# Both heads of a pair turned one behind the other in the attention loop, and latent values taken from their bank by VectorE

## The chip, the core and the metric

The kernel runs on one core of a Trainium2 chip. The metric is the device time of one execution in microseconds (us). Engines are named as the profile names them: PE is the matmul engine TensorE, PEld its weight loads, DVE is VectorE, ACT is ScalarE, POOL is GpSimd, and SP issues the DMA transfers.

## What is computed

A residual trunk of four layers over 512 tokens of width 1024: a gated short convolution, a sparse attention in which an indexer chooses 128 keys for each query (layer B below), a multi-head latent attention (layer C), and a second convolution layer. Both attention layers have 16 heads, 64-wide values, and a softmax over the visible key chunks:

```python
def attend(args):                      # dense_chunk_attention, layer C
    q_b, q0 = args
    logits = jnp.einsum("bqhd,bshd->bhqs", q_b, k).astype(jnp.float32) * scale
    mask = chunk_visible(q0 + jnp.arange(QBLOCK, dtype=jnp.int32), k_pos)
    logits = jnp.where(mask[None, None], logits, -jnp.inf)
    p = jax.nn.softmax(logits, axis=-1).astype(v.dtype)
    return jnp.einsum("bhqs,bshd->bqhd", p, v)

# mla_mixer: keys and values come out of one product of the latent vector
kv = (rmsnorm(ckv, kv_lat_norm) @ w_ukv).reshape(bsz, seq, C_HEADS, C_NOPE + C_V)
k_nope, v = kv[..., :C_NOPE], kv[..., C_NOPE:]
...
return (o * jax.nn.silu(z)) @ w_out
```

## The kernel before

Tokens lie in four blocks of 128 (`NT` = 4), features in eight blocks of 128. Weights stream in from HBM by SP (`raw`), ACT rounds them (`whi`, line 161), POOL subtracts (`wlo`, line 163), and a large product is three matmuls, high by high, low by high and high by low (lines 287 to 289).

All instructions are written in a program order, and a list scheduler lays them out on each engine: of the instructions that it takes for ready at a point of its own timeline, the one that is earliest in the program goes first. So program order is a priority and not the final order, and within an engine's queue the order is then fixed. Semaphores between engines follow from the data, and two engines that touch one PSUM bank are ordered.

`attention` (line 620) serves layers B and C. Its jobs are eight pairs of heads, and each pair is cut into six chunks: query blocks 0 and 1, then 2, then 3, for each of the two heads (even chunk: first head; odd chunk: second head). There are N = 48 chunks. The steps of a chunk are:

- `scores`: for both heads at once; score matmuls into the two `s` banks (of one buffer), then DVE (line 655, with the row maximum `mn`), then ACT's exponential with its sum (line 658).
- `normalise`: one DVE reciprocal `rc` for the pair (line 668), then the scaling of the probabilities by POOL for the first head (line 673) and by ACT for the second (line 675).
- `turn`: PE turns the probabilities, block by block, into one of two `pt` banks (line 685), and ACT copies them back (line 690), or DVE for each sixth chunk (line 688).
- `mix`: once in six chunks, 40 PE instructions (line 706) into the single `o` bank, the last chunks' probabilities first; then DVE multiplies by the gate (line 710).
- `filler`: the projections of later heads, and later gates, step by step; `filler.to(cost)` issues steps until the planned cost of a chunk is reached. `Filler` parts are generators; their own turns use the `tr` bank (line 585).

The loop at line 714 takes one chunk per round, with the scores four chunks ahead; the scores are issued in even rounds only. In a round stand, in this order, the mix, the scores, one normalise, one turn and one portion of filler.

In layer C, `keys_values` (line 1036) is part of that filler: for each block of 128 tokens, six matmuls make keys and values of four heads side by side in one bank (tag `pj`, two banks, when the loop runs; `pj` and `pt` ahead of it). `fin` takes them out: the key part by ACT with the token's factor (line 1043), the value part by ACT with the same factor (line 1044), then POOL squares the key part and DVE sums it (line 1047).

Of the kernel before, what the change touches and what calls it, by code (L numbers as in the profile page):

```python
# [13 lines left out]
AF = mybir.ActivationFunctionType  # L14
OP = mybir.AluOpType
# [56 lines left out]
def encoder(ctx: ExitStack, tc: tile.TileContext, a, out, depth=4):  # L72
# [4 lines left out]
    act_e, dve, pool, pe = nc.scalar, nc.vector, nc.gpsimd, nc.tensor  # L77
# [9 lines left out]
    def tile_of(tag, name, shape=(P, S), dtype=F32):  # L87
        return sb.tile(list(shape), dtype, name=name, tag=tag, bufs=BUFS[tag])
# [4 lines left out]
    def tiny(name, n, dtype=F32, tag="tiny"):  # L93
        return sb.tile([P, n], dtype, name=name, tag=tag, bufs=24)

    def bank(name, tag):
        return ps.tile([P, S], F32, name=name, tag=tag, bufs=BANKS[tag])

    def two_banks(name):

        b = ps.tile([P, 2, S], F32, name=name, tag="s", bufs=1)
        return [b[:, 0], b[:, 1]]
# [233 lines left out]
    def tokens_short(group, act, finish, tags):  # L336

        w = [x for _, u in units(group) for x in u]
        for t in range(NT):
            b = bank("pt", tags[t % len(tags)])  # L340
            for k in range(group.nk):
                products(b[:, :group.n], [y[:, t * P:(t + 1) * P] for y in act[k]], w[k], k == 0, k == group.nk - 1)
            finish(t, b)
            yield
# [275 lines left out]
    def attention(jobs, filler):  # L620

        early_turns[0] = False
        chunks = []
        for j in jobs:
            mine = [(j, e, ts) for ts in ([0, 1], [2], [3]) for e in range(2)]
            for i, c in enumerate(mine):
                chunks.append(c + (j["fill"][0] + (j["fill"][1] - j["fill"][0]) * (i + 1) / len(mine),))  # L630
        stage, soft, wide, factors = {}, {}, {}, {}

        def parts(ts):

            o = 0
            for t in ts:
                yield t, slice(o, o + (t + 1) * P)
                o += (t + 1) * P

        def scores(c):  # L640

            j, _, ts = chunks[c][:3]
            if ts[0] == 0:
                filler.through(j["after"])
            banks = two_banks("s")
            n = len(ts)
            for t, w in parts(ts):
                j["scores"]([b[:, w] for b in banks], t)
            ps_ = [tile_of("p", "p") for _ in range(2)]
            mn = [tiny("mn", n, tag="small") for _ in range(2)]  # L650
            sm = tiny("sum", 2 * n, tag="small")
            for e in range(2):
                p = ps_[e]
                for i, (t, w) in enumerate(parts(ts)):
                    dve.tensor_tensor_reduce(out=p[:, w], in0=banks[e][:, w], in1=j["masks"](t), scale=j["qs"](e, t),  # L655
                                             scalar=-GONE, op0=OP.add, op1=OP.min, accum_out=mn[e][:, i:i + 1])
                for i, (t, w) in enumerate(parts(ts)):
                    act_e.activation(p[:, w], p[:, w], AF.Exp, bias=mn[e][:, i:i + 1], scale=-1.0,  # L658
                                     accum_out=sm[:, e * n + i:e * n + i + 1])
                stage[c + e] = p, sm  # L660

        def normalise(c):

            e, ts = chunks[c][1:3]
            p, sm = stage.pop(c)
            if e == 0:
                rc = tiny("rc", 2 * len(ts), tag="small")
                dve.reciprocal(rc, sm)  # L668
                factors[c] = factors[c + 1] = rc
            rc = factors.pop(c)[:, e * len(ts):(e + 1) * len(ts)]  # L670
            for i, (t, w) in enumerate(parts(ts)):
                if e == 0:
                    pool.tensor_scalar(p[:, w], p[:, w], rc[:, i:i + 1], None, op0=OP.mult)  # L673
                else:
                    act_e.activation(p[:, w], p[:, w], AF.Copy, scale=rc[:, i:i + 1])
            soft[c] = p

        def turn(c):

            ts = chunks[c][2]  # L680
            p = soft.pop(c)
            b = bank("pt", "pt")
            n = sum(t + 1 for t in ts) * P
            for i in range(0, n, P):
                pe.transpose(b[:, i:i + P], p[:, i:i + P], ident)  # L685
                clock[0] += 0.11
            if c % 6 == 5:
                dve.tensor_copy(p[:, :n], b[:, :n])
            else:
                act_e.activation(p[:, :n], b[:, :n], AF.Copy)  # L690
            wide[c] = p

        def mix(c):

            j, e, ts = chunks[c][:3]
            if e == 0 or ts[-1] < NT - 1:
                return
            o = bank("o", "o")
            first = True
            for d in (4, 2, 0):  # L700
                x = [wide.pop(c - 5 + d + e) for e in range(2)]
                for t, w in reversed(list(parts(chunks[c - 5 + d][2]))):
                    for kb in range(t + 1):
                        i = w.start + kb * P
                        for e in (1, 0):
                            pe.matmul(o[64 * e:64 * e + 64, t * P:(t + 1) * P], j["v"](e, kb), x[e][:, i:i + P],  # L706
                                      start=first, stop=t == 0)
                            clock[0] += 0.134
                        first = False
            dve.tensor_tensor(j["dst"](), o, j["dst"](), op=OP.mult)  # L710

        N = len(chunks)
        ahead = 4
        for c in range(-ahead, N + 1):
            if c > 0:
                mix(c - 1)
            if c + ahead < N and c % 2 == 0:
                scores(c + ahead)
            if 0 <= c + ahead - 1 < N:
                normalise(c + ahead - 1)  # L720
            if 0 <= c < N:
                turn(c)
            if c + ahead < N:
                filler.to(chunks[c + ahead][3])
        while filler.step():
            pass
        early_turns[0] = True
# [193 lines left out]
    def layer_c(last):  # L921
# [49 lines left out]
        def factor(which, n):  # L971
            p = token_sums(sums[which])
            v = tiny("lv", NT)
            r2 = tiny("lr2", NT)
            pool.tensor_tensor(out=r2, in0=r, in1=r, op=OP.mult)
            dve.tensor_tensor(v, p[:, :NT], r2, op=OP.mult)
            y = small_rsqrt(v, NT, 1.0 / n)
            f = const([P, NT], "f" + which)
            pool.tensor_tensor(out=f, in0=y, in1=r, op=OP.mult)
            return f  # L980

        fkv = factor("kv", 256)
# [53 lines left out]
        def keys_values(g, dst, vals):  # L1036
            sums = tiny("hs", 16)
            ks = [tile_of("gate", "kk", (P, 4, 96)) for _ in range(NT)]

            def fin(t, b):  # L1040
                b3 = b.rearrange("p (h d) -> p h d", d=P)
                x3 = ks[t][:, :, :64]
                act_e.activation(x3, b3[:, :, :64], AF.Copy, scale=fkv[:, t:t + 1])
                act_e.activation(vals[t // 2][:, t % 2], b3[:, :, 64:], AF.Copy, scale=fkv[:, t:t + 1])
                q = tile_of("rp", "qk2", (P, 4, 64))
                pool.tensor_tensor(out=q, in0=x3, in1=x3, op=OP.mult)
                dve.tensor_reduce(sums[:, 4 * t:4 * t + 4], q, axis=AX.X, op=OP.add)

            yield from tokens_short(a["c_ukv"][g], lat["kv"], fin, free(g))
            v = tiny("hv", 16)  # L1050
            pool.tensor_tensor(out=by_head(v), in0=by_head(sums), in1=krs[:, :, None].to_broadcast([P, NT, 4]),
                               op=OP.add)
            y = small_rsqrt(v, 16, 1.0 / 96)
            for t in range(NT):
                x = ks[t]
                yt = y[:, 4 * t:4 * t + 4, None]
                pool.tensor_tensor(out=x[:, :, :64], in0=x[:, :, :64], in1=yt.to_broadcast([P, 4, 64]), op=OP.mult)
                pool.tensor_tensor(out=x[:, :, 64:], in0=krr[:, t, None].to_broadcast([P, 4, 32]),
                                   in1=yt.to_broadcast([P, 4, 32]), op=OP.mult)

            def finish(h):
                to_features(dst[h], lambda t: ks[t][:, h], 96)
            for h in range(4):
                finish(h)
# [152 lines left out]
```

## Time and profile before

| | us |
|---|---|
| median of 3 runs | 1058.24 (1058.1 to 1058.6) |
| profiled execution, its own time | 1058.71 |
| its span, first to last instruction | 1056.9 |
| PE busy in the span | 1044.1 |
| ACT busy in the span | 511.5 |
| DVE busy in the span | 523.6 |
| POOL busy in the span | 678.3 |

Layer B's loop lies at about 372 to 545 us of the span and layer C's at about 645 to 820 us. A row of the timeline gives the start, the length, engine, line, output and inputs, and how many instructions of one kind were merged. Matmuls overlap in the rows: PE's pace is read from start to start, not from the length of one. A row of waits says who waited for whom: the sum, how often, and the longest. The granted clock of PE was 0.998 of full speed (2.4 GHz) over the span.

### The profile page before, as it was taken

What the parts mean: (1) busy time and instruction counts of PE and PEld (TensorE: products, weight loads), DVE (VectorE), ACT (ScalarE), POOL (GpSimd) and SP (SyncE); (2) the same over time, 40 slices, a digit from 0 to 9 for tenths busy, and PEclk for the clock granted to TensorE, in tenths of its full rate; (3) what the DMA queues carried; (4) which work ended last, traced back from release to release, by engine and by line L of the source; (5) the groups of instructions that cost most, each with busy time, mean ns of one, the idle gap of its engine ahead of it and who ended that gap; (6) DMA issues with size and microseconds to landing.
All of it is one profiled execution on the core that took longest, in us unless ns stands there. A gap on an engine that the chain in (4) does not pass through costs nothing.

```text
span 1056.9 us, 16253 instructions
## 1 busy us (share of the span) xinstructions
PE 1044.1 (99%) x6040; PEld 878.9 (83%) x6040; DVE 523.6 (50%) x1074; ACT 511.5 (48%) x1091; POOL 678.3 (64%) x636
## 2 busy tenths in 40 slices
PE   9999999999999999999999999999999999999998
PEld 7888888898898999898888787687777888888886
DVE  6884334335598974443435344444442664443321
ACT  6243223434444467676644446876764533333231
POOL 1546555666378799685538689788743856555552
PEclk9999999999999999999999999999999999999999
DMA  7233333224222221111213220101211333333332
GB/s 238 93 100 100 99 99 92 83 70 120 81 71 80 72 89 41 61 56 46 71 50 105 82 83 23 41 24 60 61 55 46 100 100 101 99 100 100 100 100 79
DMA packets 27295, 86.44 MB, mean 82 GB/s; under 512 B 3408, under 2 KB 4432, under 8 KB 27216
## 3 DMA queue, kind: packets, MB, share of 16 engines
q1 hardware_dynamic: 26928, 85.10, 25.9%
q8 instruction: 47, 0.77, 0.3%
q10 hardware_dynamic: 288, 0.31, 0.1%
q14 instruction: 32, 0.26, 0.1%
HBM read 83.30 MB, written 2.10 MB: 81 GB/s over the span
## 4 chain that ended last, share of the span: by engine, by line
PE 94%; DVE 2%; ACT 1%; POOL 1%; DMA 1%; issue 1%; ACTq 0%; POOLq 0%
PE pa L287 11%; PE pa L288 11%; PE pa L289 11%; PE po L287 6%; PE po L289 6%; PE po L288 6%; PE o L706 4%; PE pt L685 4%; PE s L1083 3%; PE pz L289 2%; PE pz L288 2%; PE pz L287 2%; PE s L296 2%; PE tr L585 2%; PE pq L287 2%; PE pk L288 2%
## 5 line engine op out<-in xcount | busy, mean ns | idle before, releaser
L163 POOL TENSOR_TENSOR wlo<-raw,whi 128x512 fp32r<-128x512 f32 (+4 forms) x320 | 401.4, 1262 | 281.4 <-ACT whi L161 269.4
L161 ACT ACTIVATE whi<-raw 128x512 fp32r<-128x512 f32 (+4 forms) x329 | 196.9, 603 | 328.9 <-PE pa L288 158.4
L288 PE MATMUL pa<-xl,whi 128*128 128x512 f32 x512 | 199.3, 389 | 0.0
L287 PE MATMUL pa<-xh,whi 128*128 128x512 f32 x512 | 198.2, 389 | 0.6 <-ACT xh L370 0.6
L289 PE MATMUL pa<-xh,wlo 128*128 128x512 f32 x512 | 197.6, 389 | 0.0
L287 PEld LDWEIGHTS pa<-xh,whi 128*128 128x128 f32 x512 | 96.0, 188 | 20.6 <-ACT xh L370 0.8
L288 PEld LDWEIGHTS pa<-xl,whi 128*128 128x128 f32 x512 | 96.1, 188 | 20.5 <-DVE xl L373 0.5
L289 PEld LDWEIGHTS pa<-xh,wlo 128*128 128x128 f32 x512 | 96.1, 188 | 20.0
L673 POOL TENSOR_SCALAR p<-p,rc 128x128 f32<-128x128 f32 (+1 forms) x64 | 70.2, 1103 | 45.9 <-DVE rc L668 40.6
L658 ACT ACTIVATE p<-p,mn 128x128 f32<-128x128 f32 (+3 forms) x128 | 71.0, 558 | 17.5 <-DVE mn L655 17.3
L480 DVE TENSOR_TENSOR cg<-pa,R 128x512 f32<-128x512 f32 x16 | 11.0, 690 | 118.5 <-PE pa L289 116.2
L655 DVE CUSTOM_DVE_ANT_0 p<-s,cmask,qs 128x128 f32<-128x128 f32 (+2 forms) x80 | 37.7, 506 | 33.9 <-PE s L1083 20.0
L287 PE MATMUL pz<-xh,whi 128*128 128x512 f32 x128 | 51.4, 401 | 0.0
L289 PE MATMUL pz<-xh,wlo 128*128 128x512 f32 x128 | 50.9, 398 | 0.0
L288 PE MATMUL pz<-xl,whi 128*128 128x512 f32 x128 | 50.4, 394 | 0.0
L288 PE MATMUL po<-xl,whi 128*128 128x512 f32 x128 | 50.1, 391 | 0.0
L288 PE MATMUL po<-glo,whi 128*128 128x512 f32 x128 | 49.8, 389 | 0.0
L282 POOL TENSOR_TENSOR y<-mean,minus_half 128x16 f32<-128x16 f32 (+1 forms) x18 | 49.2, 2732 | 0.8
L287 PE MATMUL po<-xh,whi 128*128 128x512 f32 x128 | 49.5, 400 | 0.0
L287 PE MATMUL po<-ghi,whi 128*128 128x512 f32 x128 | 49.5, 389 | 0.0
L690 ACT ACTIVATE p<-pt 128x384 f32<-128x384 f32 (+1 forms) x80 | 38.6, 510 | 22.0 <-PE pt L685 21.6
L685 PE MATMUL pt<-ident,p 128*128 128x128 f32 x320 | 47.9, 277 | 0.2 <-ACT p L690 0.2
(247 smaller groups left out, 2418.8 us busy)
## 6 DMA issues: line engine op xcount, KB each, us to landing
raw<-in_a_in SPq DMA_DIRECT2D x63, 512.0 KB, 3.9
raw<-in_a_out SPq DMA_DIRECT2D x16, 512.0 KB, 3.9
raw<-in_b_z SPq DMA_DIRECT2D x8, 512.0 KB, 3.5
raw<-in_b_q SPq DMA_DIRECT2D x8, 512.0 KB, 3.4
raw<-in_b_k SPq DMA_DIRECT2D x8, 512.0 KB, 3.7
raw<-in_b_v SPq DMA_DIRECT2D x8, 512.0 KB, 3.6
raw<-in_c_z SPq DMA_DIRECT2D x8, 512.0 KB, 3.6
raw<-in_b_out SPq DMA_DIRECT2D x8, 384.0 KB, 3.3
```

The costliest lines, as they stand in the source:

```text
L161: act_e.activation(hi[:, :, c], raw[:, j:j + m, c], AF.Copy)
L163: e.tensor_tensor(out=lo, in0=raw[:, j:j + m, :n - few], in1=hi[:, :, :n - few].bitcast(F32), op=OP.subtract)
L282: pool.tensor_tensor(out=y, in0=m, in1=minus_half[:, :n], op=OP.pow)
L287: nc.tensor.matmul(o, l[0], r[0], start=first, stop=False)
L288: nc.tensor.matmul(o, l[0], r[1], start=False, stop=False)
L289: nc.tensor.matmul(o, l[1], r[0], start=False, stop=last)
L655: dve.tensor_tensor_reduce(out=p[:, w], in0=banks[e][:, w], in1=j["masks"](t), scale=j["qs"](e, t), scalar=-GONE, op0=OP.add, op1=OP.min, ...
L658: act_e.activation(p[:, w], p[:, w], AF.Exp, bias=mn[e][:, i:i + 1], scale=-1.0, accum_out=sm[:, e * n + i:e * n + i + 1])
L673: pool.tensor_scalar(p[:, w], p[:, w], rc[:, i:i + 1], None, op0=OP.mult)
L685: pe.transpose(b[:, i:i + P], p[:, i:i + P], ident)
L690: act_e.activation(p[:, :n], b[:, :n], AF.Copy)
L706: pe.matmul(o[64 * e:64 * e + 64, t * P:(t + 1) * P], j["v"](e, kb), x[e][:, i:i + P], start=first, stop=t == 0)
```

## The change

Two edits. The loop of `attention` takes both chunks of a pair in one round: it counts in steps of two, issues the scores of the pair four chunks ahead, normalises the two chunks two and three ahead, turns both chunks of the pair one behind the other, and then issues the filler up to the planned cost of the second chunk of the pair whose scores it issued. In `keys_values` the value part is taken out of its bank by DVE and no longer by ACT.

```diff
         N = len(chunks)
         ahead = 4
-        for c in range(-ahead, N + 1):
+        for c in range(-ahead, N + 1, 2):
             if c > 0:
                 mix(c - 1)
-            if c + ahead < N and c % 2 == 0:
+            if c + ahead < N:
                 scores(c + ahead)
-            if 0 <= c + ahead - 1 < N:
-                normalise(c + ahead - 1)
+            for d in (c + ahead - 2, c + ahead - 1):
+                if 0 <= d < N:
+                    normalise(d)
             if 0 <= c < N:
                 turn(c)
+                turn(c + 1)
             if c + ahead < N:
-                filler.to(chunks[c + ahead][3])
+                filler.to(chunks[c + ahead + 1][3])
         while filler.step():
             pass
         early_turns[0] = True
...
                 act_e.activation(x3, b3[:, :, :64], AF.Copy, scale=fkv[:, t:t + 1])
-                act_e.activation(vals[t // 2][:, t % 2], b3[:, :, 64:], AF.Copy, scale=fkv[:, t:t + 1])
+                dve.tensor_scalar(vals[t // 2][:, t % 2], b3[:, :, 64:], fkv[:, t:t + 1], None, op0=OP.mult)
                 q = tile_of("rp", "qk2", (P, 4, 64))
```

## Rows read from the trace of the kernel before

**Rows 1.** The page's first part: busy us, share of the span, instructions.

```profile
PE 1044.1 (99%) x6040; PEld 878.9 (83%) x6040; DVE 523.6 (50%) x1074; ACT 511.5 (48%) x1091; POOL 678.3 (64%) x636
```

**Rows 2.** Busy us by stretch: length, PE, PEld, DVE, ACT, POOL, clock, DMA.

```profile
372.00:545.00 173.00, 172.60 (x1445) 151.41 (x1443) 81.15 (x235) 114.18 (x286) 126.98 (x115) 1.00 0.19 59
645.00:820.00 175.00, 171.53 (x1094) 135.95 (x1094) 76.05 (x243) 119.92 (x314) 121.79 (x147) 1.00 0.15 44
```

**Rows 3.** Waits, whole span: who for whom, us in total, times, longest.

```profile
PE tr L585 <- ACT kT L113: 1.6, 2, 1.0
PE s L1083 <- DVE mn L655: 1.5, 2, 1.1
...
PEld pt L287 <- ACT v L1044: 0.2, 1, 0.2
...
DVE rc L668 <- ACT p L658: 34.9, 30, 2.0
```

**Rows 4.** PE's timeline in B: start, us, instruction; last-block scores, cut and whole.

```profile
424.33 0.73 PE L296 MATMUL s<-kT,qT 64*128 64x512 f32 x3
424.99 2.40 PE L706 MATMUL o<-p,v 128*64 128x128 f32 x40
427.33 0.73 PE L296 MATMUL s<-kT,qT 64*128 64x512 f32 x3
427.99 0.88 PE L685 MATMUL pt<-ident,p 128*128 128x128 f32 x6
...
484.64 0.96 PE L296 MATMUL s<-kT,qT 64*128 64x512 f32 x5
...
511.69 0.96 PE L296 MATMUL s<-kT,qT 64*128 64x512 f32 x6
512.58 0.33 PE L685 MATMUL pt<-ident,p 128*128 128x128 f32 x1
```

**Rows 5.** PE's timeline in C: a mix in two pieces.

```profile
757.76 1.09 PE L706 MATMUL o<-p,v 128*64 128x128 f32 x14
...
759.35 1.74 PE L706 MATMUL o<-p,v 128*64 128x128 f32 x26
761.02 0.55 PE L685 MATMUL pt<-ident,p 128*128 128x128 f32 x3
```

**Rows 6.** Busy us of line 706 alone: B's and C's loop, one mix of C.

```profile
372.00:545.00 173.00, 19.43 (x320) 17.26 (x320) 1.00 0.19 59
645.00:820.00 175.00, 22.23 (x320) 18.37 (x320) 1.00 0.15 44
...
712.50:720.40 7.90, 3.66 (x40) 2.49 (x40) 1.00 0.42 135
```

**Rows 7.** Chain that ended last: runs of eight turns, first and last of thirteen.

```profile
403.02 1.02 PE pt L685 x8
...
808.19 0.87 PE pt L685 x8
```

**Rows 8.** Groups by line: count, busy us, mean ns, idle before and its releaser.

```profile
L673 POOL TENSOR_SCALAR p<-p,rc 128x128 f32<-128x128 f32 (+1 forms) x64 | 70.2, 1103 | 45.9 <-DVE rc L668 40.6
L690 ACT ACTIVATE p<-pt 128x384 f32<-128x384 f32 (+1 forms) x80 | 38.6, 510 | 22.0 <-PE pt L685 21.6
...
L1044 ACT ACTIVATE v<-pt,fkv 128x256 f32<-128x256 f32 x16 | 7.4, 470 | 0.0
L1018 DVE TENSOR_TENSOR qk<-pt,gqk 128x256 f32<-128x256 f32 x16 | 6.7, 420 | 7.3 <-ACT qk L1017 7.3
```

**Rows 9.** Timeline in C's loop: ends of two key-and-value blocks, copies between.

```profile
721.64 0.39 PE L289 MATMUL pt<-whi,llo 128*128 128x512 f32 x1
...
722.07 0.47 ACT L1043 ACTIVATE kk<-pt,fkv 128x256 f32<-128x256 f32 x1 [1.40 <-PE pt L289]
...
722.44 0.46 ACT L1044 ACTIVATE v<-pt,fkv 128x256 f32<-128x256 f32 x1
...
723.00 0.39 PE L289 MATMUL pt<-whi,llo 128*128 128x512 f32 x1
```

## Prediction

> **What bounds the kernel now.** I read the busy table first: the matmul row of TensorE (PE) is busy for 1044.1 of 1056.9 us, every other engine for 64% of the span or less [rows 1]. A busy row alone does not say that the engine is at its pace, so the second view is the table by stages. The change touches two stretches: the attention loop of the sparse layer (B, 372 to 545 us) and that of the latent layer (C, 645 to 820 us). PE is without work for 173.00 - 172.60 = 0.4 us of the first and 175.00 - 171.53 = 3.5 us of the second; VectorE (DVE) is busy for under half of either, ScalarE (ACT) for two thirds [rows 2]. The third view is PE's waits: over the whole kernel the named ones are small, among them 1.5 us for DVE's `mn` (the score banks) and 1.6 us for ACT's `kT` (the `tr` bank); PE's weight loads waited 0.2 us for ACT's `v` [rows 3].
>
> So the loop is not held up by its attention chain. The scheduler fills every wait with other matmuls, those of the filler first. What such a kernel can still lose lies in the order of PE's own stream: runs of one kind that are cut in two. That is the fourth view, PE's instructions in order. In B the six score matmuls of the last query block take 512.58 - 511.69 = 0.89 us when they run through. At 424 us the scheduler puts the mix (40 instructions) into their middle: three take 424.99 - 424.33 = 0.66 us, and the other three, behind the mix, 427.99 - 427.33 = 0.66 us, so 1.32 us in all. One cut costs 0.43 us. B has four such places, at 424, 445, 465 and 485 us [rows 4]. A mix can be cut as well. Whole, as at 424.99, it is busy for 2.40 us and takes 2.34 until PE's next start [rows 4]. In C one goes through in pieces of 14 and 26, with four turns of the filler between: the pieces are busy for 1.09 + 1.74 = 2.83 us, and take 2.69 from start to next start (1.02 for the first, up to the filler's turns, and 761.02 - 759.35 = 1.67 for the second), so a cut costs some 0.36 us [rows 5]. The eight mixes of B are busy for 19.43 us, the eight of C for 22.23, against 8 x 2.40 = 19.2 [rows 6]: nearly all cuts of mixes are C's.
>
> **The change part by part.** Nothing is removed from PE: the same scores, turns, mixes and filler are issued. What moves is the program order, which gives the scheduler its priorities.
>
> *Both turns together, the filler behind them.* So far a pair's second turn stood behind one portion of filler, and the mix behind one more. Now both turns stand ahead of a double portion, and mix and scores follow it. Turns beside each other save nothing as such: thirteen runs of eight turns (five in B, eight in C) are already whole, the first of them 1.02 us from start to next start, the last 0.87 [rows 7]. What changes is how early the mix can start. Its last input is the second head's copy, and that is now due a whole double portion before it. At the four places of B the scores went first although they stand behind the mix in the program, so the scheduler took the mix for not yet ready. With the copies earlier I expect mix, then scores, unbroken: 4 x 0.43 = **1.7 us less**. Bounds: 1.7 us less at best, and 1.7 us more if instead the other four pairs of B are cut, at the same price.
>
> *Normalising one portion later.* The even head's scaling on GpSimd (POOL) now stands behind the whole portion of filler, together with the odd head's on ACT; the turn follows one double portion later, not three single ones. In the queue of POOL this puts the filler's low-part subtractions ahead of a scaling of 1.10 us. POOL stood still ahead of these scalings for 40.6 us, waiting for the reciprocal [rows 8], and DVE for 34.9 us over 30 waits ahead of the reciprocal, for the exponentials [rows 3]. Part of this goes, but PE did not wait for it, so I cost it at nothing. Its cover is the double portion, in B on average 173/24 = 7.2 us a pair; if it ran out, one scaling (1.10 us) would show per pair that it concerns.
>
> *Banks and tiles.* The two turns of a pair take both `pt` banks at once, each freed by a copy (0.51 us on ACT [rows 8]), with the 7.2 us of a pair until they are wanted again. The ten `p` tiles are handed out in the same order as before. Nothing.
>
> *Latent values by DVE.* Sixteen ACT instructions of 470 ns go (7.5 us of ACT); sixteen DVE ones come, for which the nearest row is DVE's product from the same kind of bank and width, 420 ns: 6.7 us [rows 8]. Neither engine ends anything: DVE has 99 us free in C's stretch. PE's weight loads waited 0.2 us in all for ACT's `v` [rows 3]. But the filler's key and value products, and the turns behind them, are among what cuts C's mixes when a bank or an operand from ACT comes late. The busy sum puts C's cuts at 22.23 - 19.2 = 3.0 us at most [rows 6]; but each further piece shows its modelled end twice, 0.43 us of busy time for the 0.36 of the cut above, so by starts it is 3.0 x 0.36/0.43 = 2.5 us, two fifths of it in the mix at 713 us, which goes through in five pieces and is busy for 3.66 us instead of 2.40 [rows 6]. With ACT relieved I take a fifth of it, **0.5 us less**; bounds 0 and 2.5.
>
> Sum: 1.7 + 0.5 = 2.2 us less. The profiled execution took 1058.71 us (span 1056.9 and 1.8 around it), 0.5 over the median of 1058.24. So 1056.5 for such an execution and 1056.0 for the median.
>
> **The rivals.**
>
> *A new deal of the same cards.* The scheduler breaks runs where it thinks that something is not ready, and after a shift of every priority the breaks come elsewhere. For it: the cuts follow no rule that the program states (four of B's eight last blocks ran whole, four were cut), C's stalls belong to the filler's turns, and no engine's work shrinks on the path. Against it: B's four cuts are of one kind and have one reason. Time: 1058.2, give or take 1.5.
>
> *Slower: the value copy holds the bank.* Inside the loop the filler's key and value blocks have two `pj` banks. A block is six matmuls, 723.00 - 721.64 = 1.36 us; its two ACT copies start at 722.07 and 722.44 and the second ends at 722.90, 0.83 us after the first began. The bank is needed again when the next block is through, so, with 0.1 us for the hand-over, some 0.4 us are to spare [rows 9]. With the second copy on DVE, 0.47 + 0.42 us still fits, but DVE takes its instructions in order, and ahead of `v` may stand a reciprocal that waits for an exponential (34.9/30 = 1.16 us on average [rows 3]) or the gate product that waits for a mix. Queued behind the waiting `v` are the next scores' maxima, for which the score banks wait. Eight of the sixteen copies fall into C's loop; if each came 1.16 us late, 0.76 beyond the spare time, that is 6.1 us: 1058.2 - 1.7 + 6.1 = 1062.6. It decides where `v` starts over 0.4 us behind the end of the key copy. Against it: DVE is busy 43% of that stretch. A row shows the same hand-over: DVE's query product, the first to read its bank after ACT, waited 7.3 us in all for ACT's last read of it [rows 8]. The Trainium skill (PSUM — Partial Sum Buffer, "PSUM bank collisions raise a hardware error") says that two engines must not read one bank and quadrant together, reads with reads included, so software has to order them; the trace agrees, and by this rule the two copies cannot run side by side, which is the condition of this rival.
>
> *More than forecast.* All of C's cuts and its idle time go: 1058.2 - 1.7 - 2.5 - 3.5 = 1050.5. For it: one of C's stalls is a wait for ACT. Against it: the 1.5 us for `mn` are scores waiting for the score banks [rows 3], and the scores' own order stays.
>
> That the change does not do what it says has a form too: if the scheduler pulls the turns apart again, the first rival's time holds.
>
> **How the numbers follow.** 0.2%, about what a measurement of this kernel can tell from no change, is 2.1 us: the bound lies at 1056.1, close to the forecast. Chances: forecast 0.46 (its own range 1054.6 to 1057.4, two thirds of it below the bound), new deal 0.27, slower 0.17, more 0.10. Faster: 0.31 + 0.10 = 0.41; same: 0.15 + 0.27 = 0.42; slower: 0.17. The range goes from 1052.5 (about half of the larger gain) to 1060.5 (four of the eight late copies).
>
> **What would show it.** Right: in B the six last-block scores in one run of 0.89 us behind an unbroken mix, at all eight pairs; the eight mixes of C busy for under 22 us; PE idle in B still under 1 us; `v` on DVE within 0.4 us of the key copy's end, about 420 ns long. Wrong: a new wait of PE's `pt` products for DVE's `v`, score runs cut at new places, or more idle time of PE in C than 3.5 us.

## The result, and the profile after

The changed kernel takes 1064.31 us against 1058.10 for the kernel before (medians of one session). Over all runs that count the ratio is 1.0066, 95% interval 1.0053 to 1.0079; the medians alone give 1.0059, for one run took 1068.0 us, which a median does not feel. Another of the five runs took 1734.21 us, at a granted clock of 0.556 of full speed, and is left out. The changed kernel is 6 us slower; the forecast was 2 us faster, and the time lies above the range. The profiled execution of the changed kernel took 1064.31 us with a span of 1062.5, 5.6 us over the 1056.9 of before.

The page's busy line of the changed kernel (busy us, share, instructions), which answers to [rows 1]:

```profile
PE 1043.9 (98%) x6040; PEld 877.7 (83%) x6040; DVE 527.3 (50%) x1090; ACT 503.6 (47%) x1075; POOL 679.9 (64%) x636
```

PE has the same 6040 instructions and 0.2 us less busy time. ACT lost 7.9 us and DVE gained 3.7. None of that is the 5.6 us: PE's time went into standing still. Where, is shown by the stages of the changed kernel, as in [rows 2] (length, PE, PEld, DVE, ACT, POOL, clock, DMA):

```profile
372.00:545.00 173.00, 171.57 (x1426) 150.89 (x1426) 78.75 (x235) 111.76 (x285) 127.26 (x115) 1.00 0.19 58
645.00:820.00 175.00, 166.69 (x1050) 130.62 (x1052) 76.66 (x250) 115.39 (x303) 121.95 (x146) 1.00 0.15 43
```

PE is without work for 173.00 - 171.57 = 1.4 us of B (0.4 before) and 175.00 - 166.69 = 8.3 us of C (3.5 before). That is 1.0 + 4.8 = 5.8 us more, the size of the whole loss; what is left over cancels. The granted clock is 1.00 in both.

The waits of the changed kernel, as in [rows 3] (who for whom: us in total, times, longest):

```profile
DVE p L655 <- PE o L706: 17.1, 10, 4.7
...
PE s L1085 <- DVE mn L655: 2.4, 5, 1.2
PE tr L585 <- ACT kT L113: 2.2, 4, 0.7
...
PE tr L585 <- ACT qT L113: 1.6, 3, 0.7
...
PEld pt L287 <- DVE v L1046: 1.3, 2, 0.8
...
PE po L287 <- ACT qT L113: 1.1, 1, 1.1
...
DVE rc L668 <- ACT p L658: 0.5, 2, 0.3
```

PE's own waits are still small one by one. Most of what grew is the filler's, whose turns wait for ACT's `kT` and `qT`; the scores' wait for `mn` grew too, from 1.5 [rows 3] to 2.4 us. The line that gives the cause away is the last. Before, DVE waited 34.9 us at reciprocals `rc` for the exponentials, that is, the reciprocal stood first in DVE's queue and was done the moment its sum was there [rows 3]. Now it waits 0.5 us: its sum is long there when its turn in the queue comes.

**The place of the loss.** In the kernel before, the last block of C's fourth pair goes like this (rows picked from the timeline of ACT, DVE and PE):

```profile
703.23 0.19 ACT L658 ACTIVATION_READ_ACCUMULATOR p<-p,mn 128x1 f32 x1
703.45 0.17 DVE L668 RECIPROCAL rc<-sum 128x2 f32<-128x2 f32 x1 [0.94 <-ACT p L658]
...
709.23 1.03 PE L685 MATMUL pt<-ident,p 128*128 128x128 f32 x8
...
712.93 1.09 PE L706 MATMUL o<-p,v 128*64 128x128 f32 x14
```

The reciprocal follows the exponentials' end (703.42) at once; turns and mix come while PE is busy with the filler's products. In the changed kernel the same block (rows picked from the timeline of ACT, DVE, POOL and PE):

```profile
702.69 0.19 ACT L658 ACTIVATION_READ_ACCUMULATOR p<-p,mn 128x1 f32 x1
...
712.83 0.60 PE L585 MATMUL tr<-ident,kk 128*96 128x128 f32 x4
713.18 0.47 PE L288 MATMUL pt<-wlo,lhi 128*128 128x512 f32 x1
...
715.79 0.60 PE L585 MATMUL tr<-ident,kk 128*96 128x128 f32 x4
717.07 0.64 PE L585 MATMUL tr<-ident,kk 128*96 128x128 f32 x4 [0.68 <-ACT kT L113]
718.43 0.64 PE L585 MATMUL tr<-ident,qk 128*96 128x128 f32 x4 [0.72 <-ACT kT L113]
719.76 0.64 PE L585 MATMUL tr<-ident,qk 128*96 128x128 f32 x4 [0.68 <-ACT qT L113]
720.24 0.39 PE L1085 MATMUL s<-kT,qT 96*128 96x128 f32 x2
721.08 0.64 PE L585 MATMUL tr<-ident,qk 128*96 128x128 f32 x4 [0.46 <-ACT qT L113]
...
722.96 0.35 DVE L655 CUSTOM_DVE_ANT_0 p<-s,cmask,qs 128x128 f32<-128x128 f32 x1 [2.55 <-PE s L1085]
...
724.32 0.16 DVE L668 RECIPROCAL rc<-sum 128x2 f32<-128x2 f32 x1
724.46 1.56 PE L1085 MATMUL s<-kT,qT 96*128 96x384 f32 x4 [1.20 <-DVE mn L655]
724.58 1.57 POOL L673 TENSOR_SCALAR p<-p,rc 128x512 f32<-128x512 f32 x1 [4.45 <-DVE rc L668]
726.21 1.09 PE L685 MATMUL pt<-ident,p 128*128 128x128 f32 x8 [0.19 <-POOL p L673]
...
729.30 2.40 PE L706 MATMUL o<-p,v 128*64 128x128 f32 x40
```

The exponentials end at 702.88, a little earlier than before. The reciprocal, 0.16 us of work, comes at 724.32, 21.4 us later. In the program it now stands behind the next pair's `scores`. That pair is the fifth, the first of a new group of four heads: its scores need `q` and `k` that the filler has still to project and turn (`filler.through` in `scores`), so its first score products come at 720.24 and its maxima on DVE at 722.96. DVE stands in front of these maxima for 2.55 us with the reciprocal behind them. Ahead of the maxima DVE's queue has steps of the filler, and DVE waits for their inputs as well: 5.57 us at 713.03, 0.79 at 716.52 and 3.05 at 719.99.

Meanwhile PE has run out of other work. What it has left is the filler's turns, in fours through the `tr` bank. A four takes PE 713.18 - 712.83 = 0.35 us where a product follows it; here the next four waits for ACT to empty the bank, and fours follow each other at 719.76 - 718.43 = 1.33 us. The fourth pair's last eight turns and its mix of 40 could have stood in these holes, and they are just what the reciprocal locks out. PE's idle time from 715.79 to 726.21 is 0.68 + 0.72 + 0.68 + 0.46 + 1.20 + 0.19 = 3.9 us; in the kernel before the same turns and scores show 0.46 and 1.09 us, so 2.4 us more.

The late mix holds up products of the filler, too. There are four `v` tiles, two for each group of heads, so the first two value copies of the last group write a tile that the fourth pair's mix still has to read. In the changed kernel:

```profile
717.42 0.47 ACT L1045 ACTIVATE kk<-pt,fkv 128x256 f32<-128x256 f32 x1 [0.41 <-PE tr L585]
...
731.85 0.86 DVE L1046 TENSOR_SCALAR v<-pt,fkv 128x256 f32<-128x256 f32 x2
...
733.36 0.59 PE L287 MATMUL pt<-whi,lhi 128*128 128x512 f32 x1
```

The key copies at 714.62 and 717.42 have read both `pj` banks; the value copies out of the same banks come at 731.85, when the mix is through, and the next key-and-value products only at 733.36. In the kernel before, these products ran from 717 to 723 us, where the changed kernel has its holes. That the banks are what the products waited for fits these rows and was not tested apart.

The hold comes again where the seventh pair opens the last group. There the exponentials end at 747.89 and the reciprocal starts 32.5 us later (DVE's and PE's timeline of the changed kernel):

```profile
777.12 0.64 PE L585 MATMUL tr<-ident,qk 128*96 128x128 f32 x4 [0.46 <-ACT qT L113]
...
780.36 0.16 DVE L668 RECIPROCAL rc<-sum 128x2 f32<-128x2 f32 x1
780.42 0.50 PE L287 MATMUL po<-xh,whi 128*128 128x512 f32 x1 [1.13 <-ACT qT L113]
```

PE's idle time there is 0.46 + 1.13 = 1.6 us, where before had none. The two places make 4.0 of C's 4.8 us; of the rest 0.5 lies in the first 40 us of its loop (2.4 against 1.9) and 0.4 at 800 us. In those first 40 us lies a third opening inside the loop, that of the second group by the third pair: its reciprocal is held for 3.5 us only, and PE stands still for 0.52 + 0.19 + 0.21 = 0.9 us from 679 to 682, where before had nothing (a wait of 1.0 us that before had at 667 us is gone).

### The profile page after: what moved, and what is told of

The parts are those of the page before. It is cut to its first block, busy times and chain, and to the rows that moved or that the text cites. A ratio compares the mean times of both kernels' runs of the same rounds, so it can differ in the third digit from the quotient of the medians.

```text
span 1062.5 us, 16288 instructions
## 1 busy us (share of the span) xinstructions
PE 1043.9 (98%) x6040; PEld 877.7 (83%) x6040; DVE 527.3 (50%) x1090; ACT 503.6 (47%) x1075; POOL 679.9 (64%) x636
## 4 chain that ended last, share of the span: by engine, by line
PE 92%; DVE 2%; POOL 2%; ACT 1%; issue 1%; DMA 0%; DVEq 0%; ACTq 0%; POOLq 0%
PE pa L287 11%; PE pa L288 11%; PE pa L289 11%; PE po L287 6%; PE po L288 5%; PE po L289 5%; PE o L706 4%; PE pt L685 3%; PE pz L289 2%; PE pz L288 2%; PE pz L287 2%; PE s L1085 2%; PE tr L585 2%; PE s L296 2%; PE pq L287 2%; PE pv L287 2%
## 5 line engine op out<-in xcount | busy, mean ns | idle before, releaser
L658 ACT ACTIVATE p<-p,mn 128x128 f32<-128x128 f32 (+3 forms) x128 | 71.1, 557 | 37.6 <-DVE mn L655 37.1
L289 PE MATMUL po<-xh,wlo 128*128 128x512 f32 x128 | 46.7, 392 | 0.0
```

What stands on the lines that cost most here:

```text
L289: nc.tensor.matmul(o, l[1], r[0], start=False, stop=last)
```

## The experiments

**Which edit, and in which layer.** Four kernels: the loop edit alone, the value edit alone, and the loop edit (without the value edit) in one layer only, for which `attention` got a flag.

```diff
-                dve.tensor_scalar(vals[t // 2][:, t % 2], b3[:, :, 64:], fkv[:, t:t + 1], None, op0=OP.mult)
+                act_e.activation(vals[t // 2][:, t % 2], b3[:, :, 64:], AF.Copy, scale=fkv[:, t:t + 1])
```

> The loop edit without the value copy: line 1044 stays on ACT. Theory (the loop edit leaves the filler's turns of layer C alone on PE, each waiting for ACT's copy out of the one tr bank): 1063 to 1065.5 us, PE idle in C's loop 7 to 9 us. Rival (DVE's value copy holds the pj banks): 1056 to 1059 us, PE idle in C's loop under 4.5 us.

The loop edit alone: 1065.82 us, ratio 1.0077 [1.0060, 1.0094], with 9.3 us of idle PE in C: both just above what was expected. It carries the whole loss, and a little more.

> The value copy by DVE with the loop of before. Theory: 1057.5 to 1058.8 us, PE's waits for DVE's v under 0.7 us. Rival (the value copy holds the banks): 1062 to 1064 us, PE idle in C's loop 8 us.

The value edit alone, on the loop of before: 1056.45 us, ratio 0.9985 [0.9976, 0.9995], a gain of about 1.5 us. That is faster than the theory's range, although PE's weight loads waited 1.3 us for `v`, not under 0.7; the rival's 1062 to 1064 us did not come. Line 706 alone in C (640 to 830 us for the changed kernel, 645 to 820 for the value edit), as in [rows 6], first the changed kernel, then the value edit alone:

```profile
640.00:830.00 190.00, 20.96 (x320) 17.59 (x320) 1.00 0.15 44
```

```profile
645.00:820.00 175.00, 20.73 (x320) 17.84 (x320) 1.00 0.15 44
```

Against 22.23 before, C's mixes lost 1.5 us of busy time with the value edit alone; from start to next start they take 19.90 us and not 21.12, so 1.2 us of cuts. The stretch from C's first key copy (line 1043) to the first scores of the loop takes 648.20 - 611.32 = 36.9 us with the value edit and 649.12 - 611.49 = 37.6 before: 0.7 us of gain lie ahead of the loop, where I had looked for none. The same stretch takes 36.8 us with the loop edit alone, so it is not the value copy as such that shortens it.

> The paired loop in layer B alone, the old one in C, value copy on ACT. If the loss is C's alone: 1057 to 1059 us; the gain forecast for B's uncut score runs would show as 1056.5 us. If the paired loop costs in every layer: 1060 to 1062 us.

Paired loop in B only: 1058.85 us, ratio 1.0010 [1.0000, 1.0019]. The gain forecast for B (1056.5) is not there.

> The paired loop in layer C alone, the old one in B, value copy on ACT. If the loss is C's alone: 1063 to 1065 us, with PE idle in C's loop of 7 to 9 us. If the paired loop costs in every layer: 1060 to 1062 us. If the loss needs DVE's value copy: 1057 to 1059 us.

Paired loop in C only: 1063.89 us, ratio 1.0060 [1.0045, 1.0075]. The loss is C's: 6.3 us, against 1.1 in B. Stretch C of the kernel with the paired loop in C only:

```profile
645.00:820.00 175.00, 167.78 (x1037) 131.56 (x1036) 73.49 (x241) 117.83 (x311) 121.17 (x145) 0.99 0.14 42
```

PE's idle time in C is 7.2 us; with the paired loop in B only it is 3.9.

**Which part of the loop edit.** The loop edit moves three things: the turns, the filler's portion, and the place of `normalise`. Three kernels take them apart. In the first both edits stay, and only the two normalises of a round move ahead of the scores:

```diff
-            if c + ahead < N:
-                scores(c + ahead)
             for d in (c + ahead - 2, c + ahead - 1):
                 if 0 <= d < N:
                     normalise(d)
+            if c + ahead < N:
+                scores(c + ahead)
```

> Both edits, but the two normalises of a round stand ahead of the scores instead of behind them. New theory (the pair's reciprocal now stands behind the next scores; at the first scores of a head group, which wait for the filler's turned queries and keys, DVE's queue holds it behind their maxima, so the last turns and the mix of the pair before come late and the filler's turns run uncovered): 1055 to 1058 us, and the reciprocal of the fourth pair's last block within 2 us of its exponentials. Rival (the double portion of filler, or the turns side by side, make the loss): 1062 to 1065 us.

1055.54 us, ratio 0.9974 [0.9965, 0.9983]: the loss is gone, and this kernel is 2.7 us faster than the one before, about what was forecast for the change (2.2). Of that the value edit alone brought 1.5; the difference of the two is within their intervals. Its reciprocal and the mix of the same block, and its two stretches:

```profile
706.72 0.18 ACT L658 ACTIVATION_READ_ACCUMULATOR p<-p,mn 128x1 f32 x1
706.94 0.17 DVE L668 RECIPROCAL rc<-sum 128x2 f32<-128x2 f32 x1 [1.60 <-ACT p L658]
...
715.03 1.96 PE L706 MATMUL o<-p,v 128*64 128x128 f32 x30 [0.33 <-DVE p L688]
```

```profile
372.00:545.00 173.00, 172.27 (x1446) 151.64 (x1446) 80.97 (x236) 113.48 (x285) 126.55 (x115) 1.00 0.20 59
645.00:820.00 175.00, 171.10 (x1101) 136.71 (x1100) 80.65 (x255) 118.74 (x308) 122.86 (x147) 1.00 0.15 45
```

The reciprocal again follows the exponentials within 0.1 us (706.90 to 706.94), although these end 3.5 us later than in before; the mix comes 14 us earlier than in the changed kernel, and PE's idle time in C is 3.9 us. Turns side by side and the double portion are still in it, so neither makes the loss by itself.

The second goes the other way: the loop of before, with single turns and single portions, and only the even chunks' normalise moved to where the change puts it.

```diff
-            if 0 <= c + ahead - 1 < N:
-                normalise(c + ahead - 1)
+            for d in (c + ahead - 2, c + ahead - 1):
+                if c % 2 == 0 and 0 <= d < N:
+                    normalise(d)
```

> The loop of before, one chunk per round with single portions and single turns, value copy on ACT; only the even head's normalise is moved to the place that the paired loop gives it, behind the scores of the pair two further on. New theory: 1062 to 1066 us, the reciprocal of the fourth pair's last block some 20 us behind its exponentials. Rival (double portion or turns side by side): 1057 to 1059 us.

1064.80 us, ratio 1.0062 [1.0046, 1.0079]: the move alone makes the loss. The kernel to compare it with is the loop edit alone, 1.0077 [1.0060, 1.0094], and the intervals overlap. Its rows at the fifth pair, and its stretch C:

```profile
708.62 0.18 ACT L658 ACTIVATION_READ_ACCUMULATOR p<-p,mn 128x1 f32 x1
...
721.68 0.64 PE L585 MATMUL tr<-ident,qk 128*96 128x128 f32 x4 [0.68 <-ACT qT L113]
...
726.24 0.16 DVE L668 RECIPROCAL rc<-sum 128x2 f32<-128x2 f32 x1
```

```profile
645.00:820.00 175.00, 165.74 (x1030) 130.32 (x1030) 73.30 (x241) 118.78 (x313) 120.67 (x146) 0.99 0.15 42
```

The reciprocal is held 726.24 - 708.80 = 17.4 us, the fours of turns have the same holes, and PE is idle for 9.3 us of C.

The third keeps both edits and the turns side by side, but issues the filler in single portions again, with the first head's normalise between two of them, as in the loop of before:

```diff
-            for d in (c + ahead - 2, c + ahead - 1):
-                if 0 <= d < N:
-                    normalise(d)
+            if 0 <= c + ahead - 1 < N:
+                normalise(c + ahead - 1)
             if 0 <= c < N:
                 turn(c)
                 turn(c + 1)
             if c + ahead < N:
+                filler.to(chunks[c + ahead][3])
+                normalise(c + ahead)
                 filler.to(chunks[c + ahead + 1][3])
```

> Both edits, turns side by side, but each normalise at its old place: the second head's behind the scores, the first head's between two halves of the filler portion. New theory: 1055 to 1058 us. Rival (turns side by side, or the filler behind both): 1062 to 1065 us.

1055.85 us, ratio 0.9976 [0.9966, 0.9985], as good as normalising first. So the turns side by side cost nothing, and it doesn't matter whether the reciprocal stands right ahead of the next scores or half a portion earlier, so long as it is ahead of them.

**Which rounds.** If the loss comes from the openings of the third and the fourth head group, two rounds of the 24 must carry it. In one kernel the normalises stand ahead of the scores in those two rounds only, in the other everywhere else (the condition negated). `attention` serves both layers, so the condition holds in B as well as in C:

```diff
+            opens = c + ahead in (24, 36)
-            if c + ahead < N:
+            if c + ahead < N and not opens:
                 scores(c + ahead)
             for d in (c + ahead - 2, c + ahead - 1):
                 if 0 <= d < N:
                     normalise(d)
+            if opens:
+                scores(c + ahead)
```

> Both edits stay; the two normalises stand ahead of the scores in two rounds of the 24 only, those that issue the scores of chunks 24 and 36, the first pairs of the third and the fourth head group. Theory (the loss is one of place: a reciprocal of a pair's last blocks is held on VectorE behind score maxima that wait for the projection of a new head group, 21.5 us at 703 to 724 us of the span in the changed kernel): these two rounds carry all the loss, so 1055.5 to 1057, the time of the kernel with all normalises first, and idle PE in layer C near 4 us. Rival (the later reciprocal costs something at every pair, through the scaling that follows it): two rounds of 24 give back little, so 1062 to 1064.5, and idle PE in C stays above 7 us.

1058.98 us, ratio 1.0009 [0.9999, 1.0018].

> The complement: both edits stay, the two normalises stand ahead of the scores in every round but those two that issue the scores of chunks 24 and 36. Theory: the held reciprocal is still there, so the loss stays, 1062 to 1065, and the first scaling after 703 us of the span starts about 20 us after its exponentials end. Rival (a price at every pair): 1056 to 1058, with the loss gone although the one hold is still there.

1063.39 us, ratio 1.0050 [1.0035, 1.0065]. The reciprocal of the fourth pair's last block and stretch C, in the kernel with the two rounds mended and in the one with all others mended:

```profile
701.69 0.17 DVE L668 RECIPROCAL rc<-sum 128x2 f32<-128x2 f32 x1 [0.87 <-ACT p L658]
```

```profile
645.00:820.00 175.00, 170.44 (x1090) 133.94 (x1089) 77.87 (x251) 116.11 (x304) 120.98 (x145) 1.00 0.14 43
```

```profile
723.07 0.16 DVE L668 RECIPROCAL rc<-sum 128x2 f32<-128x2 f32 x1
```

```profile
645.00:820.00 175.00, 166.89 (x1072) 131.66 (x1074) 77.64 (x250) 116.81 (x303) 122.12 (x146) 1.00 0.15 44
```

With all but the two rounds mended, the reciprocal is still held, for 14.4 us at the fifth pair, and the loss stays, as the theory had it.

The spans say how much each part is worth: 1062.5 us for the changed kernel, 1053.7 with every round mended (8.8 less), 1057.0 with the two rounds mended (5.5 less) and 1061.6 with the others mended (0.9 less); 2.4 us come only when both are mended. By the ratios it is 0.92, 0.57 and 0.16%; the 1068.0 us run of the changed kernel weighs in all three, and the intervals do not separate the last from nothing. The theory had expected the two rounds to carry everything (1055.5 to 1057), and that was too much: they carry six tenths. The two layers can be told apart by the start of C's first key copy, which dates the end of all that comes before it, and by the length of C's loop, from its first scores to the end of its last mix:

| kernel | C's first key copy, us | C's loop, us |
|---|---|---|
| before | 611.49 | 166.6 |
| changed | 612.16 | 172.7 |
| two rounds mended | 610.96 | 168.4 |
| the others mended | 612.29 | 171.3 |
| every round mended | 610.53 | 165.1 |

So 1.2 of the two rounds' 5.5 us were won ahead of C. In C's loop, which the change had made 6.1 us longer, the two rounds give back 4.3 of 7.6 us and the others 1.5. C's idle time is mostly theirs: 4.6 us with the two mended, 8.1 with only the others mended. Of the 3.3 us between 168.4 and 165.1, 2.7 lie in the 160 turns of C's probabilities (19.96 us from start to next start, against 17.27) and 0.6 in the mixes (20.51 against 19.90). Part of this is the third opening, which the condition left out: there PE is still idle for 0.9 us, and not at all with every round mended. A kernel with all three openings mended was not run.

## Why the prediction was wrong, point by point

**What bounds the kernel** held: PE. So did its sentence that the order of PE's stream decides. That the scheduler fills every wait with other matmuls did not hold: at the openings of head groups too little was left to fill with. It counted what could be won in PE's stream, the cuts, and not what covered what.

**Normalising one portion later, costed at nothing: this is the step that failed.** It looked at the queue of POOL, to which the scaling is moved behind the filler's subtractions, and at DVE's wait for the exponentials, part of which it saw go. It left out that `normalise` issues a DVE instruction too, and that the move takes this past the next pair's `scores`, whose maxima stand in DVE's queue. The sum should have read: two scores that open a head group, behind which a reciprocal waits until the new group's `q` and `k` are through, and some 2 us of holes on PE at each (2.4 and 1.6 measured). The place of `normalise` is worth more than these holes, 6.1 us by the medians when it is moved alone. The cover that it named, the double portion of 7.2 us a pair in B, is an average; at an opening in C the portion ends in the turns on whose result the scores hang, and the holds were 21.4 and 32.5 us. The 34.9 us that DVE waited for exponentials were read as time to be saved. They were a sign that the reciprocal stood at the head of its queue: 0.5 us after, 34.9 again with the normalises first.

**Turns together, 1.7 us less.** Half of the mechanism holds, and only where the normalises are in time. In the changed kernel six of B's eight last-block score runs go through uncut, one of them in 1.20 us instead of 0.89 (at 406 us). Two are cut at places that were whole before: at 384 us the filler's turns cut off the sixth product, and at 511 us the mix goes in between (PE's timeline of the changed kernel, as in [rows 4]):

```profile
425.47 0.96 PE L296 MATMUL s<-kT,qT 64*128 64x512 f32 x6
426.84 2.40 PE L706 MATMUL o<-p,v 128*64 128x128 f32 x40
...
511.10 0.73 PE L296 MATMUL s<-kT,qT 64*128 64x512 f32 x4
511.76 2.40 PE L706 MATMUL o<-p,v 128*64 128x128 f32 x40
514.09 0.50 PE L296 MATMUL s<-kT,qT 64*128 64x512 f32 x2
```

But the scores still go ahead of the mix, not behind it, so the mix did not become ready earlier, as the step had wanted. And B's idle time rose by 1.0 us. The first key copy of C's layer, in the changed kernel, then with the normalises first:

```profile
612.16 0.48 ACT L1045 ACTIVATE kk<-pt,fkv 128x256 f32<-128x256 f32 x1 [2.25 <-POOL fkv L981]
```

```profile
610.53 0.47 ACT L1045 ACTIVATE kk<-pt,fkv 128x256 f32<-128x256 f32 x1 [2.25 <-POOL fkv L981]
```

In the kernel before:

```profile
611.49 0.47 ACT L1043 ACTIVATE kk<-pt,fkv 128x256 f32<-128x256 f32 x1 [2.24 <-POOL fkv L979]
```

Counted from the first score product of B's loop (369.10 us before, 368.98 in the changed kernel, 368.88 with the normalises first), the loop edit cost 0.8 us up to there as it was made, and gains 0.7 with the normalises first, where the forecast was 1.7. With the normalises first the mix does go ahead of the scores, unbroken, at 424 and 465 us, as forecast; at 444 and 484 us the scores are still cut. Two cuts fewer at 0.43 us are 0.9 us, and B's idle time, 0.7 us against 0.4, takes some of it back.

**Banks and tiles, nothing.** With the normalises first, both `pt` banks taken at once cost nothing that shows. The `p` tiles did move: DVE's maxima waited 17.1 us for a mix to give back a tile, 10 times, against 2.1 us before and 3.6 with the normalises first. That is a follow-up of the late mixes; what it cost was not tested apart. The `v` tiles, which this step did not list, moved for the same reason: two value copies came 14.3 and 16.8 us behind their key copies, which in the kernel before they followed at once.

**Latent values by DVE, 0.5 us less.** The sign was right, the size too small: about 1.5 us. A fifth of the 2.5 us of C's cuts was taken; half of what there was went, 1.2 us by starts (1.5 of 3.0 by busy time). With 0.7 us won ahead of the loop, and 0.4 lost to more idle time of PE in C (3.9 against 3.5), that makes the gain. The instruction itself is a little longer than its nearest row in [rows 8] said, 479 ns and not 420 (groups by line of the changed kernel):

```profile
L1046 DVE TENSOR_SCALAR v<-pt,fkv 128x256 f32<-128x256 f32 x16 | 7.2, 479 | 8.6 <-ACT kk L1045 8.6
```

**The rivals.** The measured time is near that of the slower rival (1062.6), but its mechanism is refuted: the value copy alone is faster, and PE's weight loads waited 1.3 us in all for DVE's `v`. DVE's copy often waits for ACT's key copy (8 times, 8.6 us in all) and then starts at once behind it. The Trainium skill (PSUM — Partial Sum Buffer, "PSUM bank collisions raise a hardware error") wants accesses of two engines to one bank and quadrant kept apart by semaphores; the trace shows them one behind the other, 0.03 us from the key copy's end at 690.88 to the value copy's start at 690.91, and that this cost PE little here. The two value copies that did hold their banks for long waited for the late mix, and they do so with the value copy on ACT as well: 15.5 and 14.4 us with the loop edit alone. A rival with the right mechanism, an instruction held in an in-order queue, stood in the text, but for `v` and not for `rc`.

The marks that were to show it wrong all came true: more idle time of PE in C than 3.5 us (8.3), score runs cut at new places (384 and 511 us), and a wait of PE's `pt` products for DVE's `v` (1.3 us, which the faster kernels have as well, so it told nothing of the loss). Of those that were to show it right, C's mixes under 22 us came true (20.96). `v` came within 0.1 us of the key copy's end for 11 of the 16, the score runs were whole at six of eight pairs but ahead of the mix, and PE's idle time in B was not under 1 us (1.4). Most of these marks looked at the gains only.

**The range.** Its ends do not come out of the terms that it names. Four late copies at 0.76 us give 1058.2 - 1.7 + 3.0 = 1059.5, not 1060.5; half of the larger gain of 7.7 us gives 1054.4, not 1052.5. The measured time lies above either upper end.

## What to carry to other kernels

When a step is moved in program order, list each engine that it issues to and, for each, what it is moved past; then ask what the longest wait of that instruction is, not the mean. A small instruction that gives a result early (here a reciprocal of 0.16 us) belongs ahead of anything on its engine that waits for a far producer. And look at what a piece of work covers, not only at what it waits for: a long wait of an idle engine for its input can be the sign that the order is right.

## What was not expected of the hardware

DVE copied 128 x 256 values with a factor out of a bank in 479 ns, where ACT took 470 [rows 8], so moving the copy saved no time in the pair as such. That the gain is ACT's queue, free 0.47 us earlier sixteen times, fits the fewer cuts of C's mixes but was not tested apart. And four turns of 128 columns that cost PE 0.35 us amid other work followed each other at 1.33 us when only they were left, since each four waits for ACT's 0.59 us copy of the one before (idle 0.68 us at 719.76).
